# Four output tiles of a gMLP projection as seven Strassen products, with the value transpositions between them

## The chip, the cores and the metric

The kernel runs on one core of a Trainium2 chip. The metric is the device time of one execution in microseconds (us), as the median of three runs. TensorE (PE in the profile) multiplies, VectorE (DVE) and ScalarE (ACT) do elementwise work, GpSimd (POOL) does some of it, and SyncE (SP) issues nearly all transfers from HBM.

## The reference, cut to what matters

One step of a small decoder: layer 0 is a half SwiGLU, a gMLP mixer, a half SwiGLU and a gated embedding; then a shared key/value projection; then layer 1 with attention in the mixer's place. 544 token columns (512 of the prompt, 32 of the samples) go through together; the model width is 1024. Everything is float32. The mixer is

```
u, v = split(xn @ w_in, 2)            # w_in is 1024 x 2048
v = rmsnorm(v, v_norm)
s = (w_s * lower_triangle) @ v + b_s  # per group of 128 channels, along the tokens of a chunk of 128
out = (u * s) @ w_out
```

## The kernel before, in words

**Products in three passes.** A float32 operand is split into a rounded high part and a low remainder, and a product is the sum of high by high, high by low and low by high. Weights are the stationary operand (128x128), activations the moving one, 272 token columns (HT, half of 544) at a time. A plain output tile of 128 channels (`tile_mm`, `mm`, lines 273 to 300) is 8 blocks of 128 inputs, 3 passes and 2 token halves: 48 matmuls, lines 286, 290 and 292.

**Weights.** All weights go through one list of pieces in the order of use. A piece is loaded by SP into a raw tile (line 209, 512 KB), split by an ACT cast (line 242) and a DVE subtraction (line 243), and used once. Some pieces are sums or differences of raw blocks, made by DVE (line 228). `prepare` works ahead by a triple of distances: (2, 2, 4) pieces for splits, sums and loads in the mixer, (2, 3, 6) in the feed-forward blocks. Raw, split and most activation tiles come from one pool of 45 tiles of 128x1088.

**Strassen in the feed-forward blocks.** Most of the hidden layer is computed by blocks of 2 x 2 with seven products in the order 1 5 6 2 7 3 4 (`products` and `evict`, lines 522 to 563). Both the weights and the activations need extra sums; those of the activations are `forms` (line 347): per pair of input chunks two ACT scalings, three DVE subtractions and two splits, held in two tiles. That code has its order written out by hand.

**The mixer** (`gmlp`, line 618) has its order left to a planner, which reorders the instructions of each engine by modelled times. In program order: eight v tiles, each scaled out of PSUM by DVE (line 645), squared by ACT and added up by POOL (line 371); eight u tiles (`u_tile`, scaled by DVE at line 657); after the first u tile the norm of v (`rstd`, line 400: an ACT cast, a DVE subtraction, four matmuls at line 408 into the two `pb` banks of PSUM, two ACT rows at line 386, DVE lines 389 to 393, of which line 392 is the last to read the `pb` banks); `v_turn` per channel group (DVE lines 660 and 662, a small store by SP at line 663, four PE transpositions at line 666 and one at line 667 into a `ps` tile, ACT copies at lines 669 and 670); `spatial` per group (PE lines 677 and 680, DVE lines 688 to 695 and a split); then eight tiles of the output projection. PSUM holds three `ps` tiles of two banks and two `pb` banks.

The v_turns stand after u tiles 2, 2, 3, 3, 4, 5, 6, 6; the spatials after u tiles 3 to 7.

Of the kernel before, what the change touches and what calls it, by code (L numbers as in the profile page):

```python
# [26 lines left out]
ALU = mybir.AluOpType  # L27
AX = mybir.AxisListType

P = 128  # L30
# [58 lines left out]
def woven(x):  # L89

    return x.rearrange("p (a b) -> p b a", a=2)


def turns(out):

    return out.rearrange("p (b a) -> p b a", a=2)


def unwoven(out):

    return out.rearrange("p (b a) -> p a b", a=2)


def halves(x):

    return x.rearrange("p (a b) -> p a b", a=2)
# [32 lines left out]
class Builder:  # L139
# [207 lines left out]
    def forms(self, h, gcol, n, xs):  # L347

        nc = self.nc
        x = self.big()  # L350
        for a in range(2):
            nc.scalar.activation(x[:, a, :], h[2 * n + a], AF.Copy, scale=self.gain(gcol + 2 * n + a))
        t13, t24 = self.tmp(), self.tmp()
        two = lambda t: t.rearrange("p (a b) -> p a b", a=2)
        f13, f24 = self.big(F32R), self.big(F32R)
        nc.vector.tensor_tensor(two(t13), x[:, :, HT:], two(x[:, 0, :]), ALU.subtract)
        self.split_pair(f13, t13)
        nc.vector.tensor_tensor(t24[:, :HT], x[:, 1, HT:], t13[:, :HT], ALU.subtract)
        nc.vector.tensor_tensor(t24[:, HT:], x[:, 1, :HT], t24[:, :HT], ALU.subtract)
        self.split_pair(f24, t24)  # L360
        half = lambda t, b: tuple(x[:, b * HT:(b + 1) * HT] for x in t)
        f13, f24 = ((t[:, 0, :], t[:, 1, :]) for t in (f13, f24))
        return {"1": half(xs[2 * n], 0), "2": half(xs[2 * n + 1], 0), "3": half(xs[2 * n + 1], 1),
                "5": half(f13, 0), "7": half(f13, 1), "6": half(f24, 0), "4": half(f24, 1)}
    def ssq(self, acc, h, cols=slice(0, T), first=False):

        nc = self.nc
        sq = acc[:, cols] if first else self.tmp()[:, cols]
        nc.scalar.activation(sq, h[:, cols], AF.Square)  # L369
        if not first:  # L370
            nc.gpsimd.tensor_tensor(acc[:, cols], acc[:, cols], sq, ALU.add)  # L371
# [246 lines left out]
    def gmlp(self, h, box, on_chunk):  # L618
        nc, i = self.nc, self.i
        xs = self.pairs(box)  # L620
        wst = self.big()[:, 0:2, 0:512].rearrange("p a (g t) -> p a g t", t=P)
        bsb = self.big()[:, 0:2, 0:512].rearrange("p a (g t) -> p a g t", t=P)
        wss = self.tmp()
        nc.sync.dma_start(out=wst, in_=i["ws"].rearrange("p (a g t) -> p a g t", a=2, t=P))
        nc.sync.dma_start(out=bsb, in_=i["bs"].partition_broadcast(P).rearrange("p (a g) t -> p a g t", a=2))
        nc.sync.dma_start(out=wss[:NS, :NH * NS], in_=i["wss"])
        tri = self.tmp()
        nc.sync.dma_start(out=tri[:, :P], in_=i["passed"][:, C_TRI:C_TRI + P])
        for a in range(2):
            for g in range(4):  # L630
                nc.gpsimd.tensor_tensor(wst[:, a, g, :], wst[:, a, g, :], tri[:, :P], ALU.mult)
        for g in range(NH):
            nc.gpsimd.tensor_tensor(wss[:NS, g * NS:(g + 1) * NS], wss[:NS, g * NS:(g + 1) * NS],
                                    self.c[:NS, C_TRI4:C_TRI4 + NS], ALU.mult)
        rstd, sq, v = None, self.st(), []
        for c in range(NC_):
            if rstd is None:
                p, rstd = self.tile_rstd(xs, box["acc"])
            else:
                p = self.tile_mm(xs)  # L640
            if c % 2 == 0:
                vt = self.big()

            def take(p=p, vc=vt[:, c % 2, :]):
                nc.vector.tensor_tensor(halves(vc), whole(p), halves(rstd), ALU.mult)
                self.ssq(sq, vc, first=not v)
                v.append(vc)
            self.evac(take)
        m, us = [None] * NC_, {}
        vts = {}  # L650

        def u_tile(c):
            p = self.tile_mm(xs)
            if c % 2 == 0:
                us["t"] = self.big()
            us[c] = us["t"][:, c % 2, :]
            nc.vector.tensor_tensor(halves(us[c]), whole(p), halves(rstd), ALU.mult)

        def v_turn(c):
            nc.vector.tensor_tensor(v[c], v[c], rv, ALU.mult)  # L660
            vs = self.sm(NS)
            nc.vector.tensor_scalar(vs, v[c][:, SEQ:], self.gain(G_GV + c), None, ALU.mult)
            nc.sync.dma_start(out=self.o["gv"][c], in_=vs)
            t = self.ps()
            for j in range(4):
                nc.tensor.transpose(t[:, 0, j * P:(j + 1) * P], v[c][:, j * P:(j + 1) * P], self.ident)
            nc.tensor.transpose(t[:NS, 1, :P], v[c][:, SEQ:], self.ident)
            vt = self.big()
            nc.scalar.copy(vt[:, 0, :SEQ], t[:, 0, :])
            nc.scalar.copy(vt[:NS, 1, :P], t[:NS, 1, :P])  # L670
            vts[c] = (vt[:, 0, :], vt[:, 1, :])

        def spatial(*cs):
            ps = {c: self.ps() for c in cs}
            for c in cs:
                for j in range(4):
                    nc.tensor.matmul(ps[c][:, 0, j * P:(j + 1) * P], vts[c][0][:, j * P:(j + 1) * P],
                                     wst[:, c // 4, c % 4, :], start=True, stop=True)
            for c in cs:
                nc.tensor.matmul(ps[c][:, 1, :NS], vts[c][1][:NS, :P], wss[:NS, c * NS:(c + 1) * NS],  # L680
                                 start=True, stop=True)
                vts.pop(c)
            for c in cs:
                s = ps.pop(c)
                sg = self.tmp()
                g = self.gain(G_GV + c)
                b = bsb[:, c // 4, c % 4, :]
                nc.vector.scalar_tensor_tensor(
                    sg[:, :SEQ].rearrange("p (j t) -> p j t", t=P), s[:, 0, :].rearrange("p (j t) -> p j t", t=P),
                    g, b.unsqueeze(1).broadcast_to([P, 4, P]), ALU.mult, ALU.add)  # L690
                nc.vector.scalar_tensor_tensor(
                    sg[:, SEQ:].rearrange("p (b t) -> p b t", t=NQ),
                    s[:, 1, :NS].rearrange("p (b t) -> p b t", t=NQ), g,
                    b[:, :NQ].unsqueeze(1).broadcast_to([P, NB, NQ]), ALU.mult, ALU.add)
                nc.vector.tensor_tensor(sg, sg, us.pop(c), ALU.mult)
                pair = self.big(F32R)
                self.split_pair(pair, sg)
                m[c] = pair[:, 0, :], pair[:, 1, :]

        u_tile(0)  # L700
        rv = self.rstd(sq)
        u_tile(1)
        u_tile(2)
        assert self.chain is None
        v_turn(0)
        v_turn(1)
        for c, spatials, turns in ((3, (0,), (2, 3)), (4, (1,), (4,)), (5, (2, 3), (5,)), (6, (4, 5), (6, 7)),
                                   (7, (6, 7), ())):
            u_tile(c)
            for k in turns:  # L710
                v_turn(k)
            spatial(*spatials)
        for c in range(NC_):
            p = self.tile_mm(m)
            nc.vector.tensor_tensor(halves(h[c]), whole(p), halves(h[c]), ALU.add)
            on_chunk(c)
# [654 lines left out]
    def build(self):  # L1371
# [3 lines left out]
        def plain(aps):  # L1375
            for ap in aps:
                self.add_plain(ap)

        def ple_units(n):
            for c in range(NC_):  # L1380
                self.add_plain(i["wg"][n, c])
                if c < 2:
                    self.add_plain(i["wp"][n, c])

        self.ffn_pieces(0)
        plain([i["win"][NC_ + c] for c in range(NC_)] + [i["win"][c] for c in range(NC_)])
        plain(i["wout"][c] for c in range(NC_))
        self.ffn_pieces(1)
        ple_units(0)
# [87 lines left out]
def _stationary(w):  # L1477

    k, m = w.shape
    return np.ascontiguousarray(  # L1480
        w.reshape(k // P, P, m // P, P).transpose(2, 1, 0, 3).reshape(m // P, P, k // P * P))
# [5 lines left out]
    return w.reshape(k // 256, 2, P, m // 256, 2, P).transpose(3, 4, 1, 2, 0, 5).reshape(m // 256, 4, P, k // 256, P)  # L1487


def _constants():  # L1490
    c, d = np.zeros((P, NCONST), np.float32), np.zeros((P, NPASS), np.float32)
    r = np.arange(P)
# [28 lines left out]
def _arrays(x_prompt, x_sample, p_prompt, p_sample, cache_k, cache_v, cache_logf, page_table, ffn1_norm, ffn1_w1,  # L1521
# [9 lines left out]
    for w1, w3, w2, n in ((ffn1_w1, ffn1_w3, ffn1_w2, 0), (ffn2_w1, ffn2_w3, ffn2_w2, 0),  # L1531
# [10 lines left out]
    a["wp"] = np.stack([_stationary(w).reshape(2, 4, P, 2 * P).transpose(0, 2, 1, 3).reshape(2, P, 8 * P)  # L1542
                        for w in ple_w_proj])
    a["win"], a["wout"] = _stationary(gmlp_w_in[0]), _stationary(gmlp_w_out[0])
    a["wk"] = _stationary(w_kvf[:, :D])

    a["wv"] = w_kvf[:, D:2 * D].reshape(2, 4, P, 4, 256).transpose(3, 0, 2, 1, 4).reshape(8, P, 1024)
# [50 lines left out]
```

## Time and profile before

| | us |
|---|---|
| median of three runs | 1932.85 (1932.0 to 1933.58) |
| the profiled execution, its own time | 1931.65 |
| its span, first to last instruction | 1929.9 |
| PE busy in the span | 1905.2 (99%) |
| DVE busy | 1478.6 (77%) |
| ACT busy | 949.0 (49%) |
| POOL busy | 143.4 (7%) |

The span is that of the profiled execution; the time outside it is 1.75 us. A busy PE means that at least one matmul was in flight, and matmuls overlap, so that the time between the starts of two rows says more than the length of one.

### The profile page before, as it was taken

Reading aid. Unit: us, or ns where it says so; the run is one execution under the profiler, and the core shown is the slowest. Engines: PE = TensorE matmul, PEld = TensorE weight load, DVE = VectorE, ACT = ScalarE, POOL = GpSimd, SP = SyncE. Lnnn points to the kernel's source line nnn. Section 1 sums busy time; section 2 is a strip of 40 time slices with the busy share of each in tenths; the row PEclk is TensorE's granted clock in tenths of the full one; section 3 lists DMA queues with packets and bytes.
Section 4 is the critical chain, followed back from the end, with each engine's and each line's share of the span. In section 5 each row is a group of like instructions: output and inputs, shape, how many; then the busy total and the mean of one; then the engine's idle time right before and its main releaser. Section 6 shows DMA issues by size and latency. Waiting matters only on the chain.

```text
span 1929.9 us, 38975 instructions
## 1 busy us (share of the span) xinstructions
PE 1905.2 (99%) x16508; PEld 1869.9 (97%) x16508; DVE 1478.6 (77%) x1863; ACT 949.0 (49%) x1428; POOL 143.4 (7%) x190
## 2 busy tenths in 40 slices
PE   9999999999999999999999999999999999999999
PEld 8999999999999999999999999999977899999999
DVE  7878888556788888866578888887476888788874
ACT  7545444424555344454466444444374754444561
POOL 0000000400100000023000000002131300000020
PEclk9999999999999999999999999999999999999999
DMA  5233234312223232531484332323769332323431
GB/s 196 78 120 110 89 120 157 97 48 88 88 99 119 79 111 89 162 112 39 150 306 141 121 110 99 121 83 126 229 211 328 101 110 78 121 94 105 133 109 47
DMA packets 95743, 237.61 MB, mean 123 GB/s; under 512 B 11874, under 2 KB 29570, under 8 KB 95570
## 3 DMA queue, kind: packets, MB, share of 16 engines
q1 hardware_dynamic: 95426, 235.08, 36.6%
q8 instruction: 130, 2.13, 0.4%
q14 instruction: 43, 0.35, 0.1%
q10 hardware_dynamic: 144, 0.04, 0.0%
HBM read 218.65 MB, written 16.44 MB: 122 GB/s over the span
## 4 chain that ended last, share of the span: by engine, by line
PE 88%; DVE 6%; ACT 3%; issue 2%; DMA 1%; SPq 1%; POOL 0%; DVEq 0%; ACTq 0%; POOLq 0%
PE ps L539 31%; PE ps L286 15%; PE ps L292 15%; PE ps L290 15%; PE pb L539 5%; DVE big L243 2%; ACT big L242 1%; DVE big L228 1%; PE ps L892 1%; PE ps L893 1%; PE ps L894 1%; DVE big L331 1%; DVE big L497 0%; DMA tmp<-rows 0%; PE ps L1286 0%
## 5 line engine op out<-in xcount | busy, mean ns | idle before, releaser
L539 PE MATMUL ps<-big,big 128*128 128x272 f32 x5616 | 674.1, 279 | 5.9 <-DVE big L556 3.5
L539 PEld LDWEIGHTS ps<-big,big 128*128 128x128 f32 x5616 | 660.8, 189 | 7.0 <-issue 4.0
L243 DVE TENSOR_TENSOR big<-big,big 128x1024 fp32r<-128x1024 f32 (+2 forms) x537 | 587.1, 1096 | 91.0 <-ACT big L242 89.3
L242 ACT CAST big<-big 128x1024 fp32r<-128x1024 f32 (+2 forms) x537 | 484.2, 928 | 270.2 <-DVE big L228 267.7
L286 PE MATMUL ps<-big,big 128*128 128x272 f32 x2668 | 530.2, 280 | 2.9 <-ACT big L242 2.5
L292 PE MATMUL ps<-big,big 128*128 128x272 f32 x2668 | 528.3, 279 | 2.5 <-DVE big L243 2.3
L290 PE MATMUL ps<-big,big 128*128 128x272 f32 x2668 | 527.3, 279 | 0.3 <-DVE big L343 0.3
L286 PEld LDWEIGHTS ps<-big,big 128*128 128x128 f32 x2668 | 407.1, 189 | 7.8 <-ACT big L242 4.4
L292 PEld LDWEIGHTS ps<-big,big 128*128 128x128 f32 x2668 | 406.9, 189 | 4.5 <-DVE big L243 4.1
L290 PEld LDWEIGHTS ps<-big,big 128*128 128x128 f32 x2668 | 406.9, 189 | 0.7 <-DVE big L343 0.7
L371 POOL TENSOR_TENSOR st<-st,tmp 128x544 f32<-128x544 f32 (+1 forms) x63 | 87.4, 1387 | 1477.0 <-ACT tmp L369 1476.7
L228 DVE TENSOR_TENSOR big<-big,big 128x1024 f32<-128x1024 f32 x156 | 190.1, 1219 | 0.0
L578 DVE SCALAR_TENSOR_TENSOR big<-ps,big 128x544 f32<-128x544 f32 x160 | 115.3, 721 | 75.8 <-PE ps L292 75.8
L500 ACT ACTIVATE big<-big 128x544 f32<-128x544 f32 x88 | 57.9, 659 | 145.8 <-DVE big L497 144.6
L497 DVE TENSOR_TENSOR big<-big,st 128x1088 f32<-128x1088 f32 x88 | 113.6, 1293 | 3.9 <-ACT big L561 2.0
L547 ACT COPY tmp<-ps 128x544 f32<-128x544 f32 x117 | 71.5, 611 | 89.7 <-PE ps L539 89.7
L539 PE MATMUL pb<-big,big 128*128 128x272 f32 x936 | 114.8, 279 | 0.0
L539 PEld LDWEIGHTS pb<-big,big 128*128 128x128 f32 x936 | 111.3, 189 | 0.0
L342 ACT ACTIVATE big<-big,gains 128x544 fp32r<-128x544 f32 (+1 forms) x80 | 55.5, 702 | 91.3 <-DVE big L578 55.2
L331 DVE TENSOR_TENSOR big<-big,big 128x544 fp32r<-128x544 f32 (+1 forms) x112 | 79.2, 713 | 21.7 <-ACT big L330 21.5
L343 DVE SCALAR_TENSOR_TENSOR big<-big,gains,big 128x544 fp32r<-128x544 f32 (+1 forms) x80 | 64.6, 816 | 24.2 <-ACT big L342 24.2
L330 ACT CAST big<-big 128x544 fp32r<-128x544 f32 (+1 forms) x112 | 71.2, 643 | 18.9 <-DVE big L503 14.9
(218 smaller groups left out, 1388.5 us busy)
## 6 DMA issues: line engine op xcount, KB each, us to landing
big<-in_w SPq DMA_DIRECT2D x156, 512.0 KB
big<-in_w2a SPq DMA_DIRECT2D x64, 512.0 KB
big<-in_w2b SPq DMA_DIRECT2D x32, 384.0 KB
big<-in_w13p SPq DMA_DIRECT2D x16, 512.0 KB
big<-in_win SPq DMA_DIRECT2D x16, 512.0 KB
big<-in_wg SPq DMA_DIRECT2D x16, 512.0 KB
big<-in_ck SPq DMA_DIRECT2D x16, 512.0 KB
big<-in_cv SPq DMA_DIRECT2D x16, 512.0 KB
```

The source lines that it names most:

```text
L228: self.nc.vector.tensor_tensor(t, a, b, ALU.add if op == "+" else ALU.subtract)
L242: self.nc.scalar.copy(hi, src)
L243: self.nc.vector.tensor_tensor(lo, src, hi.bitcast(F32), ALU.subtract)
L286: i = nc.tensor.matmul(o, wh, xh[:, b], start=s, stop=False)
L290: nc.tensor.matmul(o, wh, xl[:, b], start=False, stop=False)
L292: nc.tensor.matmul(o, wl, xh[:, b], start=False, stop=e)
L331: self.nc.vector.tensor_tensor(pair[:, 1, cols], src, pair[:, 0, cols].bitcast(F32), ALU.subtract)
L371: nc.gpsimd.tensor_tensor(acc[:, cols], acc[:, cols], sq, ALU.add)
L497: tt(g, g, rstd.unsqueeze(1).broadcast_to([P, 2, T]), ALU.mult)
L539: nc.tensor.matmul(turns(dst[w]), a[:, c], woven(b), start=k in "152" and kp == 0 and n == 0, stop=kp == NKP - 1 and n == 2, skip_group_ch ...
L547: nc.scalar.copy(t["r" + k], t["C" if k == "5" else "A"])
L578: nc.vector.scalar_tensor_tensor(halves(h[c]), whole(out), 0.5, halves(h[c]), ALU.mult, ALU.add)
```

## The change

The u tiles 0 to 3 (512 channels) are computed by `strassen`: output channels, inputs and tokens are each cut in two, and seven products of 4 input blocks, 3 passes and 2 channel tiles take the place of the four plain tiles. Products 1, 6, 7, 4 add up in one `ps` tile (A), 5 and 3 in another (C), 2 in the two `pb` banks (B). After products 1, 5 and 6 ACT copies the running sum to SBUF; after 2, 7 and 3 DVE adds two of these; after 4 ACT copies. `u_done` then scales by the norm (one DVE instruction for two channel tiles). The activation forms are made while the v tiles 4 to 7 are computed. Two v_turns follow each of the products 2, 7, 3 and 4. The u tiles 4 to 7 stay plain, each followed by two spatials. The first half of the u weights is stored by blocks, and the distances are (2, 3, 6) during the seven products.

```diff
+    def strassen(self, xf, done):
+        nc, tt, t = self.nc, self.nc.vector.tensor_tensor, {}
+        u4 = lambda t: t.rearrange("p w (b a) -> p w a b", a=2)
+        h4 = lambda t: t.rearrange("p w (a b) -> p w a b", a=2)
+        def step(k):
+            hi, lo = self.unit()
+            self.advance()
+            if k == "2":
+                t["B"] = [self.pb()[:, :HT] for _ in range(2)]
+            elif k in "15":
+                t["A" if k == "1" else "C"] = self.ps()[:, :, :HT]
+            out = t["A" if k in "1674" else "C" if k in "53" else "B"]
+            for kp in range(NKP):
+                xh, xl = xf[kp][k]
+                for n, (a, b) in enumerate(((hi, xh), (hi, xl), (lo, xh))):
+                    for w in range(2):
+                        c = slice(512 * w + P * kp, 512 * w + P * kp + P)
+                        nc.tensor.matmul(turns(out[w] if k == "2" else out[:, w]), a[:, c], woven(b),
...
+            if k in "156":
+                t["r" + k] = self.tmp().rearrange("p (w b) -> p w b", w=2)
+                nc.scalar.copy(t["r" + k], out)
+            elif k == "2":
+                t["g"] = self.big(), self.big()
+                for w in range(2):
+                    tt(halves(t["g"][0][:, w, :HT]), unwoven(out[w]), unwoven(t["r1"][:, w]), ALU.add)
+            elif k == "7":
+                tt(h4(t["g"][1][:, :, HT:]), u4(out), u4(t["r5"]), ALU.add)
+            elif k == "3":
+                tt(h4(t["g"][0][:, :, HT:]), u4(out), u4(t["r6"]), ALU.add)
+                done(0, t["g"][0])
+            else:
+                nc.scalar.copy(h4(t["g"][1][:, :, :HT]), u4(out))
+                done(1, t["g"][1])
+        return step
...
+            if c >= 4:
+                uf.append(self.forms(h, G_MIX, c - 4, xs))
...
-        u_tile(0)
+        def u_done(a, g):
+            nc.vector.tensor_tensor(g, g, rstd.unsqueeze(1).broadcast_to([P, 2, T]), ALU.mult)
+            for w in range(2):
+                us[2 * w + a] = g[:, w]
+
+        self.ahead = (2, 3, 6)
+        step = self.strassen(uf, u_done)
+        step("1")
         rv = self.rstd(sq)
-        u_tile(1)
-        u_tile(2)
+        step("5")
+        step("6")
         assert self.chain is None
-        v_turn(0)
-        v_turn(1)
-        for c, spatials, turns in ((3, (0,), (2, 3)), (4, (1,), (4,)), (5, (2, 3), (5,)), (6, (4, 5), (6, 7)),
-                                   (7, (6, 7), ())):
+        for k, c in zip("2734", range(0, 8, 2)):
+            step(k)
+            v_turn(c)
+            v_turn(c + 1)
+        self.ahead = (2, 2, 4)
+        for c, spatials in ((4, (0, 1)), (5, (2, 3)), (6, (4, 5)), (7, (6, 7))):
             u_tile(c)
-            for k in turns:
-                v_turn(k)
             spatial(*spatials)
...
-        plain([i["win"][NC_ + c] for c in range(NC_)] + [i["win"][c] for c in range(NC_)])
+        plain(i["win"][NC_ + c] for c in range(NC_))
+        seven([i["win7"][x] for x in range(4)])
+        plain(i["win"][4 + c] for c in range(4))
```

## Rows read from the trace of the kernel before

**Rows 1.** The page, part 1: busy time, share of the span, instructions.

```profile
PE 1905.2 (99%) x16508; PEld 1869.9 (97%) x16508; DVE 1478.6 (77%) x1863; ACT 949.0 (49%) x1428; POOL 143.4 (7%) x190
```

**Rows 2.** Windows: busy us of PE, PEld, DVE, ACT, POOL; clock; DMA share.

```profile
361.20:460.30 99.10, 99.10 (x844) 97.78 (x843) 55.01 (x80) 30.28 (x49) 14.68 (x20) 1.00 0.23 71
400.00:424.40 24.40, 24.40 (x213) 24.28 (x213) 16.06 (x29) 6.37 (x11) 1.34 (x1) 1.00 0.13 31
570.00:620.00 50.00, 50.00 (x434) 50.00 (x433) 42.27 (x49) 22.59 (x31) 0.00 (x0) 1.00 0.24 75
```

**Rows 3.** Timeline of PE in the mixer: start, us, instruction and count.

```profile
399.93 0.40 PE L286 MATMUL ps<-big,big 128*128 128x272 f32 x2
...
405.49 0.40 PE L286 MATMUL ps<-big,big 128*128 128x272 f32 x2
...
406.65 0.40 PE L408 MATMUL pb<-tmp,onesr 128*128 128x272 f32 x2
...
417.07 0.60 PE L666 MATMUL ps<-consts,big 128*128 128x128 f32 x4
417.51 0.27 PE L667 MATMUL ps<-consts,big 128*32 128x128 f32 x1
```

**Rows 4.** Timeline of PE in the second feed-forward block, its first Strassen products.

```profile
535.94 2.94 PE L539 MATMUL pb<-big,big 128*128 128x272 f32 x24
538.72 5.72 PE L539 MATMUL ps<-big,big 128*128 128x272 f32 x48
546.58 11.36 PE L539 MATMUL ps<-big,big 128*128 128x272 f32 x96 [2.14 <-DVE big L556]
```

**Rows 5.** Timeline of DVE in the mixer.

```profile
397.01 1.72 DVE L243 TENSOR_TENSOR big<-big,big 128x1024 fp32r<-128x1024 f32 x1 [0.57 <-ACT big L242]
400.13 0.72 DVE L645 TENSOR_TENSOR big<-ps,st 128x544 f32<-128x544 f32 x1 [1.41 <-PE ps L292]
403.74 0.73 DVE L404 TENSOR_TENSOR tmp<-st,tmp 128x544 fp32r<-128x544 f32 x1 [2.88 <-ACT tmp L403]
...
406.33 2.35 DVE L243 TENSOR_TENSOR big<-big,big 128x1024 fp32r<-128x1024 f32 x2
408.60 0.71 DVE L389 SCALAR_TENSOR_TENSOR tmp<-st 128x544 f32<-128x544 f32 x1
409.42 0.79 DVE L392 SCALAR_TENSOR_TENSOR tmp<-pb,tmp 128x272 f32<-128x272 f32 x2
...
411.01 2.00 DVE L660 TENSOR_TENSOR big<-big,st 128x544 f32<-128x544 f32 x3
```

**Rows 6.** Timeline of ACT in the mixer.

```profile
403.06 0.65 ACT L403 CAST tmp<-st 128x544 fp32r<-128x544 f32 x1 [1.51 <-POOL st L371]
...
406.97 0.86 ACT L386 ACTIVATE st<-pb,eps 128x272 f32<-128x272 f32 x2 [1.37 <-PE pb L408]
417.82 0.59 ACT L669 COPY big<-ps 128x512 f32<-128x512 f32 x1 [9.99 <-PE ps L667]
418.30 0.25 ACT L670 COPY big<-ps 32x128 f32<-32x128 f32 x1
```

**Rows 7.** Timeline of POOL in the mixer.

```profile
396.18 1.46 POOL L371 TENSOR_TENSOR st<-st,tmp 128x544 f32<-128x544 f32 x1 [4.26 <-ACT tmp L369]
```

**Rows 8.** Lines by form, whole span: count | busy us, mean ns | idle before.

```profile
L243 DVE TENSOR_TENSOR big<-big,big 128x1024 fp32r<-128x1024 f32 x377 | 464.7, 1236 | 77.3 <-ACT big L242 76.9
L242 ACT CAST big<-big 128x1024 fp32r<-128x1024 f32 x377 | 388.6, 1043 | 270.2 <-DVE big L228 267.7 <-PE ps L539 1.6 <-DMA big<-in_w13p 0.7
L228 DVE TENSOR_TENSOR big<-big,big 128x1024 f32<-128x1024 f32 x156 | 190.1, 1219 | 0.0
L497 DVE TENSOR_TENSOR big<-big,st 128x1088 f32<-128x1088 f32 x88 | 113.6, 1293 | 3.9 <-ACT big L561 2.0
...
L356 DVE TENSOR_TENSOR tmp<-big 128x544 f32<-128x544 f32 x16 | 11.9, 744 | 5.3 <-ACT big L352 5.1
```

**Rows 9.** Waits of SP's queue, 340 to 470 us: total, times, longest.

```profile
SPq L663 <- DVE sm L662: 41.1, 4, 39.0
```

More of the change, by code (lines that the diff above doesn't have):

```diff
@@ L364, in forms @@
                 "5": half(f13, 0), "7": half(f13, 1), "6": half(f24, 0), "4": half(f24, 1)}
+    def strassen(self, xf, done):
[16 more added lines that the diff above has]
+                        nc.tensor.matmul(turns(out[w] if k == "2" else out[:, w]), a[:, c], woven(b),
+                                         start=k in "152" and kp == 0 and n == 0, stop=kp == NKP - 1 and n == 2,
+                                         skip_group_check=True)
+            if k in "156":
[14 more added lines that the diff above has]
+        return step
     def ssq(self, acc, h, cols=slice(0, T), first=False):
@@ L634, in gmlp @@
                                     self.c[:NS, C_TRI4:C_TRI4 + NS], ALU.mult)
-        rstd, sq, v = None, self.st(), []
+        rstd, sq, v, uf = None, self.st(), [], []
         for c in range(NC_):
@@ L1377, in plain, with seven @@
                 self.add_plain(ap)
+        def seven(aps):
+            d = self.seven(aps)
+            self.pieces.extend(d[k] for k in SEVEN)
         def ple_units(n):
@@ L1487, in _blocks, with _pairs @@
     return w.reshape(k // 256, 2, P, m // 256, 2, P).transpose(3, 4, 1, 2, 0, 5).reshape(m // 256, 4, P, k // 256, P)
+def _pairs(w):
+    h = w.shape[1] // 2
+    return np.stack([_blocks(w[:, :h]), _blocks(w[:, h:])], 3).reshape(4, P, 1024)
 def _constants():
@@ L1544, in _arrays @@
     a["win"], a["wout"] = _stationary(gmlp_w_in[0]), _stationary(gmlp_w_out[0])
+    a["win7"] = _pairs(gmlp_w_in[0][:, :D // 2])
     a["wk"] = _stationary(w_kvf[:, :D])
```

## The prediction

> **What bounds the kernel now.** I read the page's first part for the engine that is never idle, then windows over the mixer, then the timelines of PE, DVE and ACT around the place of the change. PE is busy for 99% of the span [rows 1], so a microsecond anywhere else counts only where PE waits for it. In the mixer, from the first v tile to the first output tile, PE is busy for all 99.10 of 99.10 us at clock 1.00, DVE for 55.01 and ACT for 30.28 [rows 2]. There is no gap to close: only fewer matmuls can shorten this stage, and any new gap is a loss. In PE's timeline the same line comes back after 48 matmuls from 399.93 to 405.49, 5.56 us, thus 0.1158 us each [rows 3]. The Strassen products of the feed-forward block have the same step: 24 matmuls from 535.94 to 538.72, 2.78 us, again 0.1158 us each [rows 4]. A matmul costs the same in either shape, so I may count them.
>
> **What is removed on PE.** Four plain tiles are 4 x 48 = 192 matmuls, seven products are 7 x 4 x 3 x 2 = 168. The difference is 24 x 0.1158 = 2.78 us, all of it on the path. The 40 transpositions, the 4 of the norm and the spatials stay. This is 0.14% of the time, and it is the ceiling of the direct gain.
>
> **What is added on DVE.** Four sums of weights at 1.22 = 4.9; three more pieces to split at 1.24 = 3.7; four forms, each 0.74 for the wide subtraction, 0.79 for two 272-wide ones (I take line 392's pair), and two splits at 0.73 as line 404, 3.0 together, 12.0 for four; evictions of products 2, 7 and 3, 0.79 + 2 x 0.72 = 2.2; two scalings at 1.29 = 2.6. Four u evictions at 0.72 go, -2.9. Sum +22.5 us [rows 5, 8]. The stage then has 77.5 us of DVE in 96.3 us, 80%. In the steady part of the second feed-forward block DVE is busy 42.27 of 50 us, 85%, and PE all 50.00 [rows 2]. So on average it is hidden behind PE.
>
> **Where DVE is dense.** From the end of the v tiles PE will need 168 matmuls, 4 of the norm and 8 v_turns at 0.55 (417.07 to 417.51 and one more of 0.11): 19.45 + 0.46 + 4.4 = 24.3 us. DVE did 16.06 us in 24.40 there before [rows 2], among it three u evictions and a bit (2.5) and three splits (3.7). In their place come seven splits (8.7), sums 7 and 3 (2.4), the evictions (2.2) and both scalings (2.6): 25.8 us, 106%, if nothing is done ahead. In the other 72 us of the stage DVE is left with 77.5 - 25.8 = 51.7 us of work, so some 20 us are free, in part ahead of this stretch. The nearest row for what happens when DVE is full is the wait of 2.14 us that a product in the second feed-forward block had for the eviction of line 556 [rows 4]. Between products 7 and 4, which share tile A, there are here a product and two v_turns, 2.78 + 1.1 us, where there the product stood alone. Bounds: 0 and two such waits, 4.3 us. I take 0.5, nearer to 0 because the load is that of the steady stretch and the planner can run transpositions or u tile 4 in between.
>
> **ACT, POOL, SP.** ACT gets three casts at 1.04, sixteen scalings and casts of the forms at about 0.65 and four copies at about 0.6: 16 us on 30 of 96, no bound. POOL has nothing new. SP loads the same sixteen pieces of 512 KB. Its queue stood 39.0 us behind a store of line 663 that waited for the norm [rows 9]; up to there program order issues fifteen pieces in either kernel (eight plus seven before; eight, four and three now), so the last u piece and the output weights wait behind the store as before. I count 0.
>
> **The norm of v and the two `pb` banks.** The one wait that the change adds by its order is that product 2 writes the banks which line 392 reads. Before, the last v tile ended at 400.1, the cast of line 403 began at 403.06 after POOL, line 404 ended at 404.47, the second pair of line 408 at 407.05, line 386 at 407.83, then DVE did two splits (2.35) before line 389 at 408.60, and line 392 ended at 410.21 [rows 3, 5, 6]: 10.1 us from the end of v. Products 1, 5 and 6 and the four matmuls of line 408 give 76 x 0.1158 = 8.8 us of cover. If the chain keeps its times product 2 waits 1.3 us; product 7 cannot stand in at once, since tile A must first be copied. Line 408 came 1.4 us later than its data, behind the u tile, so an earlier place there, or no splits before line 389, takes the wait to 0. The other way, the copy of product 1 (0.6) and one cast (1.04) can stand before line 403 on ACT: 2.95. Bounds 0 and 2.95, and I take 0.7.
>
> **The lock between DVE and POOL.** A weight split of DVE took 1.72 us instead of 1.24 where an addition of POOL ran from 396.18, and that addition lay in its path [rows 5, 7, 8]. The forms put more such DVE work beside the eight additions, and the last one leads to the norm. By the row it costs the chain about 0.5 us, which I hold to be inside the bounds just given. The Trainium skill (SBUF — State Buffer, Who interferes with whom) says that a DVE instruction with two SBUF inputs and a GpSimd instruction that reads SBUF hold a shared port by turns, the later one blocked until the other ends. By that rule the last addition could come a whole split late, and the sum would be about 0.7 us worse than by the row.
>
> **One PSUM tile for the transpositions.** Tiles A and C leave one `ps` tile, where the pairs before had two. A v_turn holds it from 417.07 to the end of line 670 at 418.55, 1.48 us, of which PE works 0.55 [rows 3, 6]. If the second of a pair stands directly behind the first, PE waits 0.93; four pairs 3.7 us. If matmuls of the next product are put between, nothing. Bounds 0 and 3.7. I take 0: the planner reorders PE by modelled times, and in the mixer before it left no gap, with u tiles, transpositions and spatials sharing three tiles. Behind such a wait all of PE is queued.
>
> **The sum.** -2.78 + 0.5 + 0.7 + 0 = -1.58 us. The profiled execution took 1931.65 and would take 1930.1; the median of the runs is 1.2 above it, and with it I forecast 1932.85 - 1.58 = 1931.3 us.
>
> **Rivals.**
> A. All waits are hidden, and the full 24 matmuls are gained: 1930.1. For it: not one gap of PE in the mixer before. Against: product 2 behind the norm, with 1.3 us less cover than the chain took.
> B. Slower: the single transposition tile. PE stands 0.93 us in each of the four pairs; with the other waits -2.78 + 3.7 + 1.2 = +2.1, 1935.0. It decides from the point where three pairs or more wait, 2.8 us against the 2.78 gained. For it: two v_turns are written one behind the other, and at 417.07 they ran that way. Against: other matmuls are ready and the planner may take them.
> C. Slower: weights just in time. A piece that is a sum goes through sum, cast and split, 1.22 + 1.04 + 1.24 = 3.5 us, longer than a product's 2.78 [rows 8]. If the pool's 45 tiles, of which the forms hold eight through most of the products and the turned values eight more, leave no room to work ahead, six steps lose 0.72 each, 4.3 us: 1932.85 - 2.78 + 4.3 + 0.7 = 1935.1, and up to 1939 where a copy of a running sum (0.6) stands before each cast. For it: DVE at 106% of the dense stretch. Against: the feed-forward block does this all the time with the same distances.
> D. Faster by more: a later wait such as the 2.14 us at 546.58 goes too, because the work behind the mixer falls otherwise: 1932.85 - 2.78 - 2.14 = 1927.9. For it only that the order is planned anew; against it that all that follows is moved by the same amount.
>
> **How the numbers follow.** The forecast has 0.48, A 0.22, B 0.10, C 0.15, D 0.05. A measurement of this kernel can tell about 0.2% from no change, 3.9 us: faster is under 1929.0, slower over 1936.7. The forecast, A and most of B and C lie between; D and a little of A are faster, 0.05; the far half of C and B with some of C's price are slower, 0.11; so 0.84 for no difference. The range goes from 1929.0 (A, and a run 1 us below the median) to 1936.5 (B, and C to its middle). The forecast's own range, with its three waits between nothing and about 2.5 us together, is 1930.1 to 1932.6.
>
> **What would show it.** PE should have 24 matmuls fewer and the stage from the first v tile to the output projection should be 99.1 - 2.78 us plus the gaps. A gap at the start of product 2 released by DVE's line 392 is the first wait, with at most 3 us; gaps before transpositions released by ACT's copies would be B; gaps before products released by casts or splits of weights, with DVE above 95% busy, would be C. If the stage is shorter by more than 2.78 us, or PE's step per matmul differs from 0.1158 in the products, the counting is wrong. If the stage is shorter and the time is not, the gain was given back behind the mixer, for which I have no term.

## The result, and the profile after

The changed kernel takes 1937.58 us (median of 14 runs, 1936.66 to 1938.87) where the kernel before took 1932.41 beside it (14 runs, 1931.26 to 1933.92): ratio 1.0026 [1.0019, 1.0033], 5.2 us slower. The forecast was 1931.3. The profiled execution has a span of 1935.1 us, 5.2 more than before, at a mean clock of 0.999.

Lines that the text names in the new kernel: 384 the matmuls of the products; 389 and 400 ACT's copies of the running sums after products 1, 5, 6 and after 4; 393, 397 and 395 DVE's evictions of 2, 3 and 7; 352, 356, 358, 359, 330 and 331 the forms (scaling, three subtractions, cast, split); 410 POOL's addition; 442 and 443 the cast and subtraction of the norm, 447 its matmuls, 428 and 431 the DVE lines of which 431 reads `pb` last; 684 the eviction of a v tile; 707 to 711 the transpositions and ACT's copies of them; 228 a weight sum, 242 and 243 a weight's cast and split.

Part 1 of the page after:

```profile
PE 1904.8 (98%) x16484; PEld 1868.2 (97%) x16484; DVE 1501.4 (78%) x1892; ACT 964.2 (50%) x1451; POOL 142.8 (7%) x190
```

Against [rows 1], PE has 24 matmuls fewer, DVE is busy 22.8 us more (forecast 22.5), ACT 15.2 more. The counting of matmuls held; that DVE's sum agrees is luck, as the section on the prediction shows. What failed is the time between the matmuls. The kernel before had no gap in the mixer [rows 2]. PE's timeline after shows eight (start, us, instruction and count; in brackets the idle time before the row, by the modelled end of the matmul ahead of it, and the line that released PE):

```profile
400.65 5.60 PE L384 MATMUL ps<-big,big 128*128 128x272 f32 x44
407.55 0.73 PE L384 MATMUL ps<-big,big 128*128 128x272 f32 x4 [1.30 <-DVE big L331]
408.14 0.50 PE L447 MATMUL pb<-tmp,onesr 128*128 128x272 f32 x2
409.76 0.73 PE L384 MATMUL ps<-big,big 128*128 128x272 f32 x4 [1.13 <-ACT big L242]
...
411.09 2.58 PE L384 MATMUL ps<-big,big 128*128 128x272 f32 x20 [0.37 <-DVE big L243]
414.64 3.02 PE L384 MATMUL pb<-big,big 128*128 128x272 f32 x24 [0.96 <-DVE tmp L431]
...
422.27 0.66 PE L707 MATMUL ps<-consts,big 128*128 128x128 f32 x4 [0.82 <-ACT big L711]
...
423.50 2.47 PE L384 MATMUL ps<-big,big 128*128 128x272 f32 x19 [0.47 <-DVE big L243]
...
427.28 2.44 PE L384 MATMUL ps<-big,big 128*128 128x272 f32 x19 [0.64 <-DVE big L395]
...
432.54 0.66 PE L707 MATMUL ps<-consts,big 128*128 128x128 f32 x4 [0.60 <-ACT big L400]
```

Together 6.29 us. Each costs more than its idle: a matmul lasts about 0.28 us, yet the next one starts 0.1158 us after it [rows 3], so a gap also loses the overlap of 0.16; and four matmuls right behind a gap took 0.73 where 0.28 + 3 x 0.1158 = 0.63. A ninth delay hides in the first row: 44 matmuls would take 0.28 + 43 x 0.1158 = 5.26 us and took 5.60, almost without idle time. The bill is checked over the whole stage, from DVE's first eviction of a v tile to its first of the output projection. Before (start, us, instruction):

```profile
366.09 1.41 DVE L645 TENSOR_TENSOR big<-ps,st 128x544 f32<-128x544 f32 x2
...
467.68 0.72 DVE L715 TENSOR_TENSOR big<-ps,big 128x544 f32<-128x544 f32 x1 [1.61 <-PE ps L292]
```

That is 101.59 us. After it is 366.81 to 473.58 (rows below), 106.77 us: 5.18 more. With 24 x 0.1158 = 2.78 saved, 7.96 us were lost on balance: 6.29 of idle, and 1.67 of lost overlap and restarts, about 0.2 for each of eight gaps. (Row by row more is lost: the stretch from 400.65 to the first plain u tile at 433.81 takes 33.16 us where the prediction counted 24.3, 8.9 more. About 0.8 us of that comes back at the spatials, which stand in four groups instead of five.) The 5.18 us are the whole difference of the medians (5.17); none of the price stands behind the mixer. In this execution the stage also begins 0.72 us later than in the one before (366.81, not 366.09), and 0.7 us is made up again behind the mixer. That is not the change's doing: e3 and e10 below, with the same program up to there, begin the stage at 365.82 and 365.89. Where single times of the two kernels are compared, 0.72 us is this shift.

Why the products wait is seen in DVE. Windows of the kernel before (busy us of PE, PEld, DVE, ACT, POOL; clock; DMA share), beside v tiles 0 to 3 and from there to 430 us, where after has its products:

```profile
361.00:384.00 23.00, 23.00 (x201) 23.00 (x200) 9.79 (x12) 7.24 (x10) 9.30 (x16) 1.00 0.29 93
384.00:430.00 46.00, 46.00 (x397) 45.69 (x397) 26.33 (x41) 14.13 (x23) 5.58 (x4) 1.00 0.16 50
```

The same of after:

```profile
361.00:384.00 23.00, 23.00 (x201) 23.00 (x200) 9.68 (x12) 8.01 (x12) 10.02 (x17) 1.00 0.08 24
384.00:430.00 46.00, 40.24 (x333) 38.45 (x332) 44.16 (x62) 24.53 (x38) 5.80 (x4) 1.00 0.16 49
```

DVE is idle for 13 of the first 23 us in both kernels. After, it is full from 384 on, 44.16 of 46.00 us, 96%. Nothing of the added work moved into the free stretch: the planner put each form right behind its own v tile. DVE's timeline after shows how a full queue reaches PE:

```profile
366.81 1.41 DVE L684 TENSOR_TENSOR big<-ps,st 128x544 f32<-128x544 f32 x2
...
385.62 0.44 DVE L358 TENSOR_TENSOR tmp<-big,tmp 128x272 f32<-128x272 f32 x1
386.10 1.46 DVE L359 TENSOR_TENSOR tmp<-big,tmp 128x272 f32<-128x272 f32 x1
...
399.83 0.71 DVE L331 TENSOR_TENSOR big<-tmp,big 128x544 fp32r<-128x544 f32 x1
400.46 1.21 DVE L228 TENSOR_TENSOR big<-big,big 128x1024 f32<-128x1024 f32 x1
401.60 0.71 DVE L331 TENSOR_TENSOR big<-tmp,big 128x544 fp32r<-128x544 f32 x1
402.24 0.71 DVE L684 TENSOR_TENSOR big<-ps,st 128x544 f32<-128x544 f32 x1
402.87 1.21 DVE L243 TENSOR_TENSOR big<-big,big 128x1024 fp32r<-128x1024 f32 x1
404.15 0.73 DVE L356 TENSOR_TENSOR tmp<-big 128x544 f32<-128x544 f32 x1
404.91 1.47 DVE L358 TENSOR_TENSOR tmp<-big,tmp 128x272 f32<-128x272 f32 x1
406.42 0.44 DVE L359 TENSOR_TENSOR tmp<-big,tmp 128x272 f32<-128x272 f32 x1
406.78 0.72 DVE L331 TENSOR_TENSOR big<-tmp,big 128x544 fp32r<-128x544 f32 x1
...
409.18 0.72 DVE L443 TENSOR_TENSOR tmp<-st,tmp 128x544 fp32r<-128x544 f32 x1
...
414.05 0.79 DVE L431 SCALAR_TENSOR_TENSOR tmp<-pb,tmp 128x272 f32<-128x272 f32 x2
...
473.58 0.72 DVE L763 TENSOR_TENSOR big<-ps,big 128x544 f32<-128x544 f32 x1 [1.56 <-PE ps L292]
```

From 399.83 to 414.05 DVE goes from one instruction to the next (from 400 to 418 it is busy for 17.72 of 18.00 us). The last v tile is evicted at 402.24, where the kernel before did it at 400.13 [rows 5], 1.4 us later without the shift: two splits of form 2 and a weight sum stand in front. So form 3 begins at 404.15 and its split at 406.78 ends when PE, after 44 matmuls of the first products, can go on at 407.55 with four that need form 3. The rest follows at this distance. The norm's line 431 starts at 414.05 where it was 409.42 [rows 5], 3.9 us later without the shift. The cast of a split (line 242), for which PE waits until 409.76, comes late because DVE's sum before it did (ACT's timeline after):

```profile
408.67 1.99 ACT L242 CAST big<-big 128x1024 fp32r<-128x1024 f32 x2 [0.58 <-DVE big L228]
```

Part of DVE's load comes from POOL. In each form one 272-wide subtraction took about 1.46 us where its twin took 0.44, and POOL's addition ran at that moment (POOL's timeline after):

```profile
385.79 1.47 POOL L410 TENSOR_TENSOR st<-st,tmp 128x544 f32<-128x544 f32 x1 [4.21 <-ACT tmp L408]
...
404.74 1.35 POOL L410 TENSOR_TENSOR st<-st,tmp 128x544 f32<-128x544 f32 x1 [5.13 <-ACT tmp L408]
```

The subtraction that starts at 386.10 ends at 387.56, 0.30 us after POOL's addition has ended at 387.26. Four forms lose about 1.0 us each so, 4 us of DVE time. The Trainium skill (SBUF — State Buffer, Who interferes with whom) calls the port pair that DVE and GpSimd share an exclusive lock. These rows agree with it: the subtraction ends only after the addition.

### The profile page after: what moved, and what is told of

It is laid out like the page before. It is cut to its first block, busy times and chain, and to the rows that moved or that the text cites. A ratio compares the mean times of both kernels' runs of the same rounds, so it can differ in the third digit from the quotient of the medians.

```text
span 1935.1 us, 38993 instructions
## 1 busy us (share of the span) xinstructions
PE 1904.8 (98%) x16484; PEld 1868.2 (97%) x16484; DVE 1501.4 (78%) x1892; ACT 964.2 (50%) x1451; POOL 142.8 (7%) x190
## 4 chain that ended last, share of the span: by engine, by line
PE 69%; DVE 6%; ACT 2%; issue 1%; DMA 1%; POOL 0%; SPq 0%; DVEq 0%; ACTq 0%; POOLq 0%
PE ps L578 23%; PE ps L286 11%; PE ps L292 11%; PE ps L290 11%; PE pb L578 4%; DVE big L243 2%; ACT big L242 1%; DVE big L228 1%; PE ps L940 1%; PE ps L941 1%; PE ps L942 1%; DMA tmp<-rows 1%; DVE big L331 0%; PE ps L1334 0%; DMA big<-in_cv 0%
## 5 line engine op out<-in xcount | busy, mean ns | idle before, releaser
L578 PE MATMUL ps<-big,big 128*128 128x272 f32 x5616 | 674.1, 279 | 5.6 <-DVE big L595 3.5
L578 PEld LDWEIGHTS ps<-big,big 128*128 128x128 f32 x5616 | 660.8, 189 | 6.7 <-issue 4.0
L286 PE MATMUL ps<-big,big 128*128 128x272 f32 x2604 | 518.1, 280 | 3.6 <-ACT big L242 2.8
L292 PE MATMUL ps<-big,big 128*128 128x272 f32 x2604 | 516.2, 280 | 2.6 <-DVE big L243 2.5
L290 PE MATMUL ps<-big,big 128*128 128x272 f32 x2604 | 515.2, 279 | 0.0
L286 PEld LDWEIGHTS ps<-big,big 128*128 128x128 f32 x2604 | 398.0, 189 | 8.2 <-ACT big L242 4.4
L292 PEld LDWEIGHTS ps<-big,big 128*128 128x128 f32 x2604 | 397.7, 189 | 4.7 <-DVE big L243 4.2
L290 PEld LDWEIGHTS ps<-big,big 128*128 128x128 f32 x2604 | 397.6, 189 | 0.4 <-DVE big L343 0.3
L228 DVE TENSOR_TENSOR big<-big,big 128x1024 f32<-128x1024 f32 x160 | 195.0, 1218 | 0.0
```

The costliest lines, as they stand in the source:

```text
L228: self.nc.vector.tensor_tensor(t, a, b, ALU.add if op == "+" else ALU.subtract)
L286: i = nc.tensor.matmul(o, wh, xh[:, b], start=s, stop=False)
L290: nc.tensor.matmul(o, wh, xl[:, b], start=False, stop=False)
L292: nc.tensor.matmul(o, wl, xh[:, b], start=False, stop=e)
L578: nc.tensor.matmul(turns(dst[w]), a[:, c], woven(b), start=k in "152" and kp == 0 and n == 0, stop=kp == NKP - 1 and n == 2, skip_group_ch ...
```

## The experiments

Three theories. **T1**: the forms beside v tiles 4 to 7 fill DVE's queue just when the products begin; moved earlier they cost nothing. **T2**: the single `ps` tile for the transpositions, and the banks altogether, hold PE. **T3**: the chain of a summed weight (sum, cast, split) is too long for a product's 2.78 us. Each result below is the median in us, then its ratio to the kernel before, measured beside it, with the 95% interval.

**e1_forms_early**: the forms beside v tiles 0 to 3.

```diff
-            if c >= 4:
-                uf.append(self.forms(h, G_MIX, c - 4, xs))
+            if c < 4:
+                uf.append(self.forms(h, G_MIX, c, xs))
```

> Three theories of the 5.2 us. T1, DVE is full: the four activation forms stand beside v tiles 4 to 7, DVE has no spare time from 384 to 430 us, and PE waits for whatever is next in DVE's queue. T2, banks: the one PSUM tile left for the transpositions, the two pb banks and tile A make PE wait whatever DVE does. T3, the weights' chain of sum, cast and split is longer than a product, whatever else DVE does. Here the four forms are made beside v tiles 0 to 3, nothing else changes. T1: the waits shrink by most of their 8 us, 1931 to 1934 us. T2 and T3: no change, 1936.5 to 1938.5 us.

1932.53 us against 1932.05 of the kernel before, ratio 1.0002 [0.9992, 1.0012]. Its windows, as above, and then PE's waits in the mixer (engine, tile and line that waited, releaser: total us, times, longest):

```profile
361.00:384.00 23.00, 23.00 (x201) 23.00 (x200) 21.12 (x29) 15.85 (x23) 10.14 (x14) 1.00 0.21 70
384.00:430.00 46.00, 42.94 (x367) 41.76 (x366) 38.00 (x49) 23.56 (x41) 7.07 (x5) 1.00 0.27 91
```

```profile
PE pb L384 <- DVE tmp L431: 1.6, 1, 1.6
PE ps L707 <- ACT big L711: 1.0, 2, 0.7
PE ps L384 <- DVE big L395: 0.5, 1, 0.5
```

The forms now fill the stretch that was empty, and PE has still all of its 23.00 us there. The waits for lines 331, 242 and 243 are gone, with the four summed weights and their chains still in place, which speaks against T3. Two lines of program order are worth nearly 5 us. ACT carries a part of the forms too, but from 384 to 430 us it is busy for 23.56 us here and for 24.53 in the change, so the move didn't work by freeing ACT. What changed is DVE's backlog when the products begin. The last v tile in e1's timeline of DVE, and then windows of the change and of e1 behind it:

```profile
400.26 0.72 DVE L684 TENSOR_TENSOR big<-ps,st 128x544 f32<-128x544 f32 x1 [0.17 <-PE ps L292]
```

```profile
402.00:418.00 16.00, 12.17 (x95) 11.14 (x95) 15.72 (x20) 10.71 (x16) 1.35 (x1) 1.00 0.30 93
402.00:418.00 16.00, 14.41 (x125) 14.20 (x124) 15.15 (x20) 6.69 (x11) 1.69 (x1) 1.00 0.17 60
```

In e1 DVE waits for that tile; in the change the tile waited for DVE. From then on DVE is nearly full in both, but in e1 it is not behind. The lock between DVE and POOL is still there (line 359 at 371.52 took 1.47 us) and costs PE nothing, since DVE has the time.

**e2_no_forms**: no forms at all; the products read plain halves of the activations.

```diff
-                uf.append(self.forms(h, G_MIX, c - 4, xs))
+                half = lambda t, b: tuple(x[:, b * HT:(b + 1) * HT] for x in t)
+                n = c - 4
+                uf.append({k: half(xs[2 * n + (k in "2364")], int(k in "374")) for k in SEVEN})
```

> The forms are left out (12 us of DVE, 11 us of ACT): every product reads plain halves of the inputs, so u tiles 0 to 3 aren't those of the reference; matmuls, weights, evictions and transpositions stay. T1: PE's waits go but for about 1 us, 1930 to 1932.5 us. T2: the waits for ACT's copies, line 431 and the evictions stay, 3 us, 1934 to 1935.5 us. T3: the waits for casts and splits of weights stay, about 2 us, 1933 to 1934.5 us.

1931.76 us, ratio 0.9996 [0.9986, 1.0006], with the waits of e1 (1.5, 1.0, 0.5). So with the forms early, having them costs less than can be told from nothing.

**e3_one_turn**: one transposition after each of 2, 7, 3 and 4, the others after u tiles 4 and 5.

```diff
-            v_turn(c)
-            v_turn(c + 1)
+            v_turn(c // 2)
...
             u_tile(c)
+            if c < 6:
+                v_turn(2 * c - 4)
+                v_turn(2 * c - 3)
```

> One v_turn instead of two after each of the products 2, 7, 3 and 4; the other four stand after u tiles 4 and 5. T2: the two waits for the transposition tile (1.4 us) go and product 2 to 4 follow closer, 1935 to 1936.2 us. T1: DVE is as full in that stretch, but for four multiplications less (2.8 us), of which PE may get a part: 1935.5 to 1938 us. T3: 1937 to 1938 us.

1936.52 us, ratio 1.0021 [1.0011, 1.0030]: 4.5 us slower than before where the change was 5.2 slower, a difference inside the intervals. The wait for line 400 (0.60 us) is gone, the one for ACT's copies (0.82) is still there, and the waits for DVE stand as in the change. So this edit took away only a part of what T2 blames; e5 and e10 test it further. T2 alone doesn't explain the 5 us.

**e4_before_forms**: the kernel before, with forms made at v tiles 4 to 7 that nobody uses.

```diff
+            if c >= 4:
+                self.forms(h, G_MIX, c - 4, xs)
```

> The kernel before, with the four forms made beside v tiles 4 to 7 and their results not used: the load alone, without the products. T1: DVE is full only up to the end of the v tiles, there are no sums and evictions behind, and the u tiles need little of DVE: 1932 to 1933.5 us. If the forms alone make the norm late (they and POOL's additions lock each other out), the transpositions come late and PE waits: 1934 to 1936 us.

1933.4 us, ratio 1.0004 [0.9995, 1.0014], with 0.3 us of waits. The last v tile is evicted late here too, at 401.93, and DVE is full for longer than I had expected:

```profile
402.00:418.00 16.00, 16.00 (x139) 15.88 (x138) 15.44 (x23) 6.25 (x11) 1.43 (x1) 1.00 0.00 1
```

So a full DVE with a backlog costs PE next to nothing by itself. It costs time where PE's next work needs what stands in that queue: the forms, sums, splits and evictions of the products.

**e5_early_pb**: e1, and the odd transpositions go into the two `pb` banks.

```diff
-            t = self.ps()
+            if c % 2:
+                t0, t1 = self.pb(), self.pb()
+            else:
+                t = self.ps()
+                t0, t1 = t[:, 0, :], t[:, 1, :]
...
```

> On the kernel with early forms (1932.5 us; PE still waits 1.6 us for line 431 before product 2, 1.0 for the copies out of the transposition tile, 0.5 for the eviction of product 7): every second v_turn turns into the two pb banks instead of the one free ps tile. If the tile is what makes PE wait there, its two waits go and nothing else moves: 1931 to 1931.7 us. If the copies on ACT are late anyway, the wait moves to the next product: 1932 to 1933 us.

1929.63 us (10 runs, 1928.51 to 1930.74) against 1931.89, ratio 0.9987 [0.9977, 0.9996]: 2.3 us faster than before, the best version of the study, and faster than I had expected (1931 at best). One wait is left in the mixer:

```profile
PE pb L384 <- DVE tmp L431: 1.6, 1, 1.6
```

Against the kernel before, e1 is 0.5 us slower and e5 2.3 us faster: with DVE's queue free, T2's place is worth 2.7 us. In the profiled executions 2.0 us of it are seen in the mixer: its first eviction of the output projection moves from 468.14 to 466.11, as three gaps with 1.47 us of idle time go, with their restarts.

**e10_pb_only** has this edit without the early forms.

> The changed kernel (1937.6 us) with only the second turn of each pair in the pb banks, forms beside v tiles 4 to 7 as before. If the single transposition tile is a cause of its own, its two waits (0.8 and 0.6 us, 0.2 to restart each) go: 1935.3 to 1936.2 us. If DVE's queue is the bound of the whole stretch, the time comes back at its next wait: 1936.5 to 1938 us.

1936.62 us, ratio 1.0023 [1.0014, 1.0032]: 4.8 us slower than before against the change's 5.2, which is no gain that can be told from none. The mixer shows none either: its stage takes 107.11 us (365.89 to 473.00), 0.34 more than in the change. DVE's waits are those of the change, and at the transpositions four waits of 1.6 us together have taken the place of two with 1.4. With DVE late, the banks are second in line: what is taken away there comes back at the next wait.

**e6_early_sums**: e1, and from v tile 5 on the sums are made six pieces ahead.

```diff
+            if c == 5:
+                self.ahead = (2, 6, 6)
```

**e7_early_both** joins this to e5, and **e8_both_split3** has besides the splits three pieces ahead, (3, 6, 6) and (3, 3, 6).

> On the kernel with early forms: from v tile 5 on the sums of weights are made six pieces ahead instead of two or three, so that the four sums (4.9 us of DVE) lie beside the v tiles and not between the norm's steps. If the norm is late because sums stand before its steps in DVE's queue, the wait of 1.6 us before product 2 goes: 1930.5 to 1931.3 us. If it is late because of ACT, POOL and the place of line 408's matmuls in PE's order, it stays: 1932 to 1933 us.

> Both edits on the kernel with early forms. If PE's waits are separate causes that add up, only the 0.5 us for product 7 is left of 3.1, and the gain of 2.78 us shows: 1929.5 to 1930.5 us, 1.5 to 2.5 us under the kernel before. If DVE's queue only serves the next late piece instead, 1931 to 1932.5 us.

> The same with splits three pieces ahead instead of two during v tiles 5 to 7 and the products. If DVE's late work in the stretch is what is left, 0.3 to 0.7 us less than with two: 1929 to 1930 us. If tiles run short, loads or forms come late and it is 1 us or more slower than with two.

e6 takes 1932.02 us, ratio 1.0000 [0.9991, 1.0009], the time of e1. e7 takes 1932.71, ratio 1.0001 [0.9992, 1.0010], 3.1 us more than e5 and slower than either expectation; e8 takes 1935.01, ratio 1.0015 [1.0006, 1.0024], another 2.3 more. More distance gained nothing on e1 and lost on e5. DVE's timeline of e6 shows why:

```profile
397.03 0.71 DVE L686 TENSOR_TENSOR big<-ps,st 128x544 f32<-128x544 f32 x1
397.67 1.21 DVE L243 TENSOR_TENSOR big<-big,big 128x1024 fp32r<-128x1024 f32 x1
398.80 2.37 DVE L228 TENSOR_TENSOR big<-big,big 128x1024 f32<-128x1024 f32 x1
401.09 3.48 DVE L243 TENSOR_TENSOR big<-big,big 128x1024 fp32r<-128x1024 f32 x3
404.50 0.71 DVE L686 TENSOR_TENSOR big<-ps,st 128x544 f32<-128x544 f32 x1
```

Line 686 is here the eviction of a v tile. The last one stands behind a sum and three splits and comes at 404.50, where e1 had it at 400.26. (The sum took 2.37 us instead of 1.22; POOL's addition began at 398.64.) The wait for the norm is gone, but ACT squares that tile and copies product 1 the later, and PE waits 1.7 us for line 389 instead and 1.1 at two transpositions: 2.8 in all, against 3.1 in e1. T3's cure gains nothing, since the same queue carries the urgent work. That tiles ran short in e8 is not shown.

**e9_order**: e5 with the products in the order 1 5 6 3 7 2 4, so that the one that needs `pb` comes later (the scaling of the first tile moves behind product 2 to match).

```diff
...
-        for k, c in zip("2734", range(0, 8, 2)):
+        for k, c in zip("3724", range(0, 8, 2)):
...
-            self.pieces.extend(d[k] for k in SEVEN)
+            self.pieces.extend(d[k] for k in "1563724")
```

> On the kernel with early forms and every second turn in the pb banks (1929.6 us, PE waits only 1.6 us, before product 2 for line 431): the products in the order 1 5 6 3 7 2 4, so that two more products lie between the norm and product 2. If the norm's chain is all that is late, the wait goes: 1927.7 to 1928.6 us, 4 us under the kernel before. If the later eviction of product 2, the transpositions in the banks it needs, or tile A make new waits: 1929 to 1931 us.

1929.91 us, ratio 0.9988 [0.9979, 0.9997], the time of e5. The wait for line 431 is gone and others have come:

```profile
PE ps L384 <- ACT tmp L389: 0.9, 1, 0.9
PE pb L712 <- ACT big L715: 0.4, 1, 0.4
PE ps L711 <- ACT big L715: 0.3, 1, 0.3
```

Products 3 and 7 each add to a tile that ACT must first copy (line 389), and they now follow sooner; the wait was moved, not removed.

**e11_no_sums**: the change, with the four sums of weights left out.

```diff
+            a11, a21, a22, a12 = d["1"]["src"], d["5"]["sum"][0], d["4"]["src"], d["2"]["src"]
+            for k, x in (("5", a21), ("6", a22), ("7", a11), ("3", a12)):
+                d[k].update(src=x, sum=None)
```

> The changed kernel with the four sums of weights left out (products 5, 6, 7 and 3 read raw blocks, so u tiles 0 to 3 aren't those of the reference); the forms stay beside v tiles 4 to 7. T1, DVE's queue is what is late: 4.9 us less of DVE between 400 and 418 us, after the forms; the first wait, for the fourth form, stays in part, the others shrink: 1933 to 1935 us. T3, the chain sum, cast, split: the waits for casts and splits (2 us and their restarts) go and the others stay: 1934.5 to 1935.5 us, with DVE as full as before up to 430 us. If neither the sums nor their place matters: 1937 to 1938 us.

1933.06 us, ratio 1.0004 [0.9994, 1.0014]: four sums of 1.22 us less on DVE give back 0.22%, 4.3 us, most of what the change had lost. In the profiled executions the stage takes 103.70 us instead of 106.77. The first wait, for line 331, falls from 1.30 to 0.87 us, those for 242 and 243 from 1.97 to 0.47 together; the rest stays or moves. This edit takes load off DVE and shortens the chain of T3 at once, so alone it doesn't part the two; e1 does, which keeps the chain. Together they say that it helps whichever part of DVE's late work is taken out.

**e12_forms_middle**: the forms beside v tiles 2 to 5.

```diff
-            if c >= 4:
-                uf.append(self.forms(h, G_MIX, c - 4, xs))
+            if 2 <= c < 6:
+                uf.append(self.forms(h, G_MIX, c - 2, xs))
```

> The changed kernel with the forms beside v tiles 2 to 5, between the place that cost 5 us (4 to 7) and the one that cost nothing (0 to 3). T1: DVE has 6 us more to do its queue by 400 us than with the forms at 4 to 7 (two v tiles need 4 us of it), so the waits for the fourth form and the weights go and those for the norm and the one tile stay: 1932 to 1934 us. If only the very first place helps, for the loads or the tiles held: 1935 to 1937.5 us.

1934.21 us, ratio 1.0011 [1.0001, 1.0020], between the places 0 to 3 (1932.5) and 4 to 7 (1937.6), and between my two expectations. The waits are those of e1 and 0.2 us more, but the one for line 431 has become 3.17 us (the last v tile is evicted at 402.20, 1.9 us later than in e1), and after it PE is slow. PE's timeline, then windows of this run:

```profile
412.81 3.09 PE L384 MATMUL pb<-big,big 128*128 128x272 f32 x12 [3.17 <-DVE tmp L431]
```

```profile
413.00:415.00 2.00, 2.00 (x9) 2.00 (x10) 1.86 (x3) 0.73 (x2) 0.00 (x0) 0.50 0.00 0
415.00:417.00 2.00, 2.00 (x10) 2.00 (x10) 1.07 (x3) 0.00 (x0) 0.00 (x0) 0.50 0.00 0
417.00:419.00 2.00, 2.00 (x13) 2.00 (x12) 2.00 (x5) 0.00 (x0) 0.00 (x0) 0.62 0.00 0
419.00:421.00 2.00, 2.00 (x19) 2.00 (x19) 2.00 (x4) 0.00 (x0) 0.00 (x0) 1.00 0.00 0
```

Twelve matmuls took 3.09 us where twelve of product 2 took 1.66 right behind the same wait in e5, and 1.55 without one: clock 0.50, the lower of the two levels, 1.2 GHz. By these windows the clock takes 2.8 us (half of 4.00 and 0.38 of 2.00) in this execution, whose own time, 1935.86, is the longest of ten; what the other nine lost by it is not known.

## Why the prediction was wrong

It said no difference, with 1931.3; the result is slower. The price stood under rival C ("up to 1939"), but for another reason than the one given there, so that agreement is luck.

- **24 matmuls fewer, -2.78 us.** Right: the number, the step of 0.1158 in rows without a delay (28 matmuls from 417.49 in 3.41 us, 0.28 + 27 x 0.1158 = 3.41), and e5, which is 2.3 us faster than before.
- **22.5 us more on DVE.** Right by luck (22.8). Busy time counts rows that overlap only once; added up row by row, DVE's instructions are 25.3 us more. The lock made the 272-wide subtractions of the four forms 7.7 us instead of the 3.2 that I had. The three more splits of weights added 2.7, not 3.7, because splits that met POOL before (1.72 us [rows 5]) no longer did (1.23 at 389.23 and 395.43).
- **"Where DVE is dense", 0.5 us.** This is the step that failed. I found 106% for the stretch of the products "if nothing is done ahead", and then counted "some 20 us are free, in part ahead of this stretch". Some 13 of them are free from 361 to 384, but nothing moves into them: a form needs only activations that lie ready, yet its place in program order is behind v tile 4 or later, and the planner left it there. The dense stretch was not 24 us long but 46, from the first form on, with DVE at 96%. Its price: waits for lines 331, 242, 243 and 395, 3.9 us in five gaps, with the restart 4.9, beyond the bound of 4.3. With it the terms as measured come to the result: -2.78 + 4.9 + 1.2 for the norm + 1.8 for the transpositions = 5.1. e1 shows the cause, as moving the forms alone gives nearly 5 us back, and e11 from the other side; e4 shows that the full queue alone would not have done it. (The bound came from products 7 and 4, with "a product and two v_turns" between them. In program order there are four v_turns; product 4 still waited 0.64 us for the eviction of 7.)
- **The steady feed-forward stretch as a likeness.** There DVE at 85% [rows 2] left no wait for PE, so I took 0.5 "nearer to 0". At 96%, with a backlog of forms ahead of the splits and evictions that PE waits for, the likeness doesn't hold.
- **The lock, "about 0.5 us".** I priced the last addition, which leads to the norm. DVE was held up in every form, 1.0 us each, and POOL's last addition was not (1.35 us), so the late last addition that the prediction allowed for did not come. In e1 the same lock costs nothing, so it is a load on DVE, not a wait of its own.
- **Norm and `pb`, 0.7 us.** 0.96 measured at the place that I named, within the bounds. It is that short while PE is late already: with the early gaps gone it is 1.6 (e1, e5), and 3.17 in e12, above my bound of 2.95.
- **One tile for the transpositions, 0.** Wrong: 0.82 for the copy of the turn before, and 0.60 for the copy of product 4 (line 400). Putting half of the turns into `pb` gives nothing that can be told with DVE full (e10), and 2.7 us with DVE free (e5). Rival B was right in its mechanism, but it is not what decided.
- **Rival C.** It named a full DVE and gaps released by casts and splits of weights, and both are seen. But it gave as the reason the length of the chain and the lack of room to work ahead. With the forms early, working ahead farther (e6, e7, e8) made it no better; that the pool's room would have been a limit is not shown. Nor did a copy of a running sum stand before each cast, on which the 1939 rested: the casts waited for DVE's sums (0.58 us in the row of ACT above). The cover was gone because work had been put in the wrong place.
- **Behind the mixer.** Rival D did not come, and no term was needed there: the stage accounts for the whole difference.

Left open: the last 1.6 us in e5. e9 takes that wait away and gets others of the same size; whether any order of these products has none was not tried.

## What to carry to other kernels

Added work on an engine that is on average free must be placed, not only summed: look at its busy time in windows ahead of the new work and beside it, and ask which of them program order lets the work use, and what stands behind it in the queue that the bottleneck needs soon. Work whose inputs are early belongs early, ahead of the stretch in which the same engine serves the bottleneck. And look in that order: with the queue late, removing the second limit (here the banks) shows no gain; once the queue is free, the same edit is worth 2.7 us.

## What the runs showed of the hardware

- Gaps of PE up to 1.58 us left the granted clock at 1.00 (after and e5). The gap of 3.17 us in e12 was followed by 0.50, and 1.00 came back about 6 us after its end. In e8, after 2.22 us, it was 0.50 from 408 to 410 and 0.71 from 410 to 412, then 1.00. By these windows the clock took 2.8 us after the first and 1.6 after the second (half of 2 and 0.29 of 2): in these two executions a long wait cost 0.7 to 0.9 of its length again.
- A DVE subtraction of 272 columns that met POOL's addition took 1.46 us instead of 0.44, and a weight's split in e1 (at 402.75, beside POOL's addition from 401.93 to 403.69) 2.02 instead of 1.23.
